# Moving the scaled sum of the fetched V rows from ScalarE and GpSimd to one VectorE instruction

## The chip, the core and the metric

The kernel runs on one core of one Trainium2 chip. The metric is device time in microseconds (us) of one execution. The engines are named PE (TensorE: matrix products; PEld is its weight load), DVE (VectorE), ACT (ScalarE), POOL (GpSimd) and SP (SyncE, which only issues DMAs here). Each engine runs its own instructions strictly in the order in which the program lists them.

## What is computed

One layer of a decoder: two mixing branches, an expert mixer called PEER and an embedding step, over 544 tokens of width 2048. The change lies in PEER. Cut to it, the reference is:

```python
q = (xt @ w_q).reshape(n, PEER_HEADS, 2, D_KEY // 2)
s = jnp.einsum('nhpd,hpkd->nhpk', q, sub_keys)
...                                   # top 16 of 128 keys, twice; top 16 of their sums: idx, g
hb = jax.nn.gelu(jnp.einsum('chkd,cd->chk', u[ib], xb))
return jnp.einsum('chk,chkd->cd', (hb * gb), v[ib])
```

Each token picks 16 experts in each of 8 heads, 128 picks out of 16384 experts. A pick's row of `u` is dotted with the token, the result goes through a gelu and is multiplied by the pick's gate, and the pick's row of `v`, scaled by that number, is added to the token's output.

## The kernel before

The 544 tokens are columns. All weights go through one pipeline of 764 units (`run_units`), a unit being a 128 x 1024 block of weights. SP loads it (tile `wr`), ACT rounds it to a high part `wh` (L224), DVE subtracts to get the low part `wl` (L225), both two units ahead of PE, and PE runs 8 k-tiles with three products each (L280 where 416 columns are used, L284 for 544). `wh` and `wl` have three buffers each.

PEER treats the tokens in two ways. The first 416 (`DC`) meet all experts in dense products: 256 units with U (the U stage), then 256 units with V (the V stage). In the U stage an epilogue per pair of units multiplies on DVE (L1092), takes a gelu on ACT (L1093) and stores to `Hd`. The last 128 tokens (`NS`) have their rows fetched: for each of the 128 picks POOL issues an indirect DMA (L1039) that brings one row of `u` per token, 128 x 2048 numbers, and later one of `v`. A U row is multiplied with the tokens and summed on DVE (L1046, into column i of `hsp`). A V row is scaled by `hsp` on ACT (L1052) and added into `vacc` on POOL (L1053) for picks below 96. For the last 32 picks one DVE instruction does both (L1055). V rows of a batch of 32 come one batch behind U rows, one of each in turn. The fetched rows have three buffers. They lie in the tile `raw` in the U stage and in `gb` in the V stage; a V row's sum always goes to `vacc`, which is part of `raw`.

Beside the dense U products runs other side work: top-16 searches on DVE (`tk1`), the choice of the picks (`tk2`), and for the dense tokens the building of a gate table. One step of that table compares on DVE (tiles `ob` and `oa`, L997 and L999), multiplies `ob` twice by the gates on POOL (L1001), runs 8 small products on PE (L974, into a PSUM tile `aux` with two buffers), and copies them out on ACT (L976, into `gst`). After 8 steps ACT sends `gst` (2 MB) to `Gd` in memory.

The order of all this is fixed when the program is built. `run_units` calls `side()` twice per unit. Each call is a tick. It adds `pace["sp"]` to a debt, and when the debt reaches 1 a fetched row is used (`sp_step`). It adds `pace["main"]` (in us of DVE work) to another debt and runs steps of the side work, each with a cost written beside its `yield` (0.5 where none stands), until that debt is used up. What `sp_step` returns is taken off the same debt. `PACE_U` holds the two numbers for the U stage, `PACE_V` those for the V stage, where the first is so large that it never limits. 24 units before the end of the U stage `gates_done` runs whatever side work is left at once.

Of the kernel before, what the change touches and what calls it, by code (L numbers as in the profile page):

```python
# [17 lines left out]
P = 128  # L18
D = 2048
KT = D // P  # L20
NP = 512            # prompt tokens
NB, ND = 8, 4       # sample batch, tokens per sequence
T = NP + NB * ND    # token columns: prompt, then (b, t)
HB = T // 2
LP = 568            # columns of the recurrence layout: prompt, 3 spare, then (b, 7)
LH = LP // 2
RN = 8              # recurrence tiles
EPS = 1e-6
NEG = -1e30
NS = P              # last token columns, whose experts' rows are fetched one by one  # L30
DC = T - NS         # token columns that meet all experts in dense products
TC = 32             # tokens per chunk of the gate scratch
NCH = DC // TC
NW = 24             # operand pairs of the second PEER product
QB = 4
# [5 lines left out]
GS = 32768.0  # L41
PACE_U, PACE_V = (1.256, 0.243), (1e6, 0.34)
NWA = 2 * KT * T // (2 * DC)    # of these, the pairs that lie in the activations' space


def _token_tiles(t0, t1):
    """Tiles of nt tokens with ng head groups on the partitions: row = group * nt + token."""
    out = []
    while t0 < t1:
        nt = next(n for n in (128, 64, 32) if n <= t1 - t0)  # L50
        out.append((t0, nt, P // nt))
        t0 += nt
    return out
# [13 lines left out]
def _build(ctx, tc, nc, I, O):  # L67
# [9 lines left out]

# [1 line left out]
    def const(name, shape):  # L79
# [15 lines left out]

# [1 line left out]
    AH, AL = [None] * KT, [None] * KT  # L97
# [16 lines left out]

    # sum of squares of the raw columns, folded to 1/rms of every column on every partition
    ssum = {}

    def sq_add(k, pool, x=0):
        """x: whose sum it joins, VectorE's or GpSimd's (which squares for itself)"""
        new = x not in ssum  # L120
        if new:
            ssum[x] = misc[:, (4 + x) * T:(5 + x) * T]
        s = ssum[x] if new else pool.tile([P, T], F32, name="sq", tag=f"sq{x}", bufs=2 - x)
        if x:
            GP.tensor_mul(s, raw[:, k, :], raw[:, k, :])
        else:
            A.activation(s, raw[:, k, :], AF.Square)
        if not new:
            (GP if x else V).tensor_add(ssum[x], ssum[x], s)
# [12 lines left out]

# [1 line left out]
    LOADA, SPLITA = 4, 2  # L144
# [3 lines left out]
    def side():  # L148
        """A part of the work beside the products: steps worth pace["main"] us of the vector engine."""
        SPS["tick"] = SPS.get("tick", 0) + 1  # L150
        owed["sp"] += pace["sp"]
        if owed["sp"] >= 1:
            owed["sp"] -= 1
            owed["main"] -= sp_step()
        owed["main"] = min(owed["main"] + pace["main"], 2 * pace["main"])
        while owed["main"] > 0:
            c, more = advance()
            owed["main"] -= c
            if not more:
                break  # L160
# [4 lines left out]
    def unit(src, groups, **kw):  # L165
        """src: [128, 8, 128]; groups: (accumulator key, [(kl, operand getter)], start, stop, epilogue)"""
        units.append(dict(src=src, groups=groups, **kw))

    def gemm(src, ops, epi, nk=2, cols=None, **kw):
        """One output tile: nk half chunks of 8 k tiles, operands ops(k)."""  # L170
        key = object()
        for hc in range(nk):
            last = hc == nk - 1
            unit(src(hc), [(key, [(kl, (lambda k=hc * 8 + kl: ops(k))) for kl in range(8)], hc == 0, last,
                            epi if last else None)], cols=cols, **(kw if last else {}))
# [3 lines left out]
    def advance():  # L179
        cost, more = 0.0, bool(active or gens)  # L180
        while len(active) < maxact[0] and gens:
            if gens[0] is None:      # what follows needs everything before it
                if active:
                    break
                gens.popleft()
                continue
# [111 lines left out]

# [1 line left out]
    pa = ExitStack()  # L300
# [29 lines left out]

    # RG-LRU branch
    L = {}
# [9 lines left out]
    def decay_rate():  # L342
        # sp4 = 4 * softplus(-lam), with log1p kept accurate for small arguments
        t = [pL.tile([P, RN], F32, name=f"sp{i}") for i in range(6)]
# [95 lines left out]

    # attention branch
    Q = {}
# [189 lines left out]

# [1 line left out]
    W = I["w_in"]  # L634
# [10 lines left out]

# [1 line left out]
    pld = [dram.tile([P, T], F32, name=f"pl{j}") for j in range(KT)]  # L647
    plx = []

    def start_ple():  # L650
        for k in range(2):
            t = pL.tile([P, T], F32, name="pin", tag="pin", bufs=2)
            SP.dma_start(out=t, in_=I["pT"][k])
            h, l = act_tile(KT - 2 + k)      # free until the last operands of w_in are split
            split_to(h, l, t)
# [42 lines left out]

# [1 line left out]
    B = {}  # L700
# [48 lines left out]
    Hd = [dram.tile([P, DC], F32, name=f"Hd{e}") for e in range(P)]  # L749
    NGB = 3             # buffers of fetched rows  # L750
    idx, gsp, hsp = (cst.tile([P, P], dt, name=nm)
# [54 lines left out]

# [1 line left out]
    def epi_pq(j, acc):  # L808
# [44 lines left out]
    def tk1(ti, q):  # L853
# [16 lines left out]
        V.tensor_copy(TK["x1f"][:, 2 * q:2 * q + 2], x1)  # L870
        # pairs (a, b) of ranks with (a + 1)(b + 1) <= 16 hold the 16 best: a = 0, then 1..7 with b < 8,
        # then 8..15 with b = 0, in the order of the flat index
        cd = pU.tile([P, 2, 80], F32, name="cd", tag="cd", bufs=2)
# [12 lines left out]
    def tk2(ti):  # L886
# [4 lines left out]
        x1f, ts, sel = TK["x1f"][:, :nh], TK["ts"][:, :nh], TK["sel"][:, :nh]  # L891
        # ranks (a, b) of every pick, from its place among the pairs
        hu = pU.tile([P, 2, P], U32, name="hu", tag="hu", bufs=1)
# [16 lines left out]
        yield 2.4  # L910
        # the chosen key pair of every pick
        for x in range(2):
            for h2 in range(0, nh, 2):
# [11 lines left out]
                yield 1.8  # L925
        # gates
        g = pk[:, 2, :n].rearrange("p (h j) -> p h j", h=nh)
# [19 lines left out]
        for x in range(3):  # L947
            if ng == 1:
                PE.transpose(ps[:, 0, x * P:x * P + nt], pk[:, x, :], ident)
                continue  # L950
            # rows (group, token) to rows (group, pick): every group's picks in columns of its own
            ex = pU.tile([P, ng, n], F32, name="ex", tag="ex", bufs=2)
# [8 lines left out]
        yield  # L961
        # a gate, times GS to keep it in float16's range, as the sum of two float16
        g16 = pU.tile([P, P], F16, name="g16", tag="mk", bufs=1)
# [46 lines left out]

    # the fetched experts: one pick of every row of a sparse tile at a time, the rows of U against the
    # tokens on the vector engine, those of V, a batch later, into the sums on GpSimd
    BT = 32
# [29 lines left out]
    def sp_use():  # L1043
        kind, i, t, _ = fl.popleft()
        if kind == "u":
            V.scalar_tensor_tensor(t, t, 1.0, xtok, op0=ALU.mult, op1=ALU.mult, accum_out=hsp[:, i:i + 1])  # L1046
            if i % BT == BT - 1:
                b = slice(i - BT + 1, i + 1)
                A.activation(hsp[:, b], hsp[:, b], AF.Gelu_apprx_tanh)
                V.tensor_mul(hsp[:, b], hsp[:, b], gsp[:, b])  # L1050
        elif i < P - BT:
            A.activation(t, t, AF.Copy, scale=hsp[:, i:i + 1])  # L1052
            GP.tensor_add(vacc, vacc, t)  # L1053
        else:
            V.scalar_tensor_tensor(vacc, t, hsp[:, i:i + 1], vacc, op0=ALU.mult, op1=ALU.add)  # L1055

    def sp_step():
        sp_issue()
        cost = 0.0
        if fl and SPS["tick"] - fl[0][3] >= TKD:  # L1060
            cost = 2.3 if fl[0][0] == "u" else 0.0
            sp_use()
# [86 lines left out]
    def wfirst():  # L1149
        """Products for the first group; the operands that fit beside U's."""  # L1150
        gload(0)
# [17 lines left out]
    def wsecond():  # L1169
        """In place of the first half of U's operands."""  # L1170
        drain()
# [31 lines left out]
    def weave(n=3):  # L1203
        """The first halves of the last n tiles, then the second halves."""
        units[-2 * n:] = units[-2 * n::2] + units[1 - 2 * n::2]
# [32 lines left out]

    # operands of the last product go where the last group's W leave room, in the order that they leave
    def klass(p):  # L1240
# [27 lines left out]
    def post_first(g, lo, hi):  # L1268
        """The first halves of the last tiles are through: their operands' place is free."""
        def f():  # L1270
# [38 lines left out]

# [1 line left out]
    def pre_c(j):  # L1311
# [137 lines left out]
```

## Time and profile before

| | |
|---|---|
| time, median of 3 runs | 4259.7 us (4259.34 to 4266.0) |
| span of the profiled execution | 4266.4 us |
| PE busy in the span | 4122.2 us (97%) |
| DVE busy | 2807.7 us (66%) |
| ACT busy | 1534.6 us (36%) |
| POOL busy | 1224.6 us (29%) |
| U stage (1516.7 to 2901.0 us) | 1384.3 us |
| V stage (2901.0 to 4065.0 us) | 1164.0 us |

The profiled execution's own time is its span, 6.7 us above the median. PE is the engine that the rest feeds, so the table's first question is where PE is idle or runs at less than the full granted clock, and the second is which engine's instruction ended that idle time. Both stages multiply the same number of 416-column products, so their difference is a first measure of what PE loses in the U stage.

### The profile page before, as it was taken

What the parts mean: (1) busy time and instruction counts of PE and PEld (TensorE: products, weight loads), DVE (VectorE), ACT (ScalarE), POOL (GpSimd) and SP (SyncE); (2) the same over time, 40 slices, a digit from 0 to 9 for tenths busy, and PEclk for the clock granted to TensorE, in tenths of its full rate; (3) what the DMA queues carried; (4) which work ended last, traced back from release to release, by engine and by line L of the source; (5) the groups of instructions that cost most, each with busy time, mean ns of one, the idle gap of its engine ahead of it and who ended that gap; (6) DMA issues with size and microseconds to landing.
All of it is one profiled execution on the core that took longest, in us unless ns stands there. A gap on an engine that the chain in (4) does not pass through costs nothing.

```text
span 4266.4 us, 63247 instructions
## 1 busy us (share of the span) xinstructions
PE 4122.2 (97%) x26089; PEld 4024.8 (94%) x26089; DVE 2807.7 (66%) x3659; ACT 1534.6 (36%) x1799; POOL 1224.6 (29%) x723
## 2 busy tenths in 40 slices
PE   7999999999999999999888988889999999999999
PEld 7999999999999999999878988889999999999999
DVE  7755444233434369888887988757888878877443
ACT  4442334321223233343343344334444444332331
POOL 3000000000000001464485377413555555410000
PEclk9999999999999999999999999999999999999999
DMA  5232232243343347677666666668989888997333
GB/s 180 80 125 79 75 106 86 84 135 134 124 131 104 111 144 266 234 274 254 215 231 213 233 209 217 224 221 289 332 312 332 326 315 314 323 327 248 118 131 102
DMA packets 323154, 848.69 MB, mean 199 GB/s; under 512 B 26409, under 2 KB 170729, under 8 KB 290097
## 3 DMA queue, kind: packets, MB, share of 16 engines
q1 hardware_dynamic: 204960, 492.69, 34.3%
q0 software_dynamic: 44864, 295.20, 18.6%
q10 hardware_dynamic: 73040, 56.76, 4.0%
q8 instruction: 204, 3.34, 0.3%
q14 instruction: 86, 0.70, 0.0%
HBM read 760.78 MB, written 83.77 MB: 198 GB/s over the span
## 4 chain that ended last, share of the span: by engine, by line
PE 85%; DVE 9%; ACT 2%; issue 2%; DMA 1%; ACTq 1%; POOL 0%; SPq 0%; DVEq 0%
PE acc L280 45%; PE acc L284 36%; DVE wl L225 4%; DVE raw L1046 1%; PE aux L974 1%; ACTq L1094 1%; ACT wh L224 1%; DVE misc L1092 1%; PE aux L519 1%; ACT gst L976 1%; PE aux L556 1%; DMA Gd<-gst 0%; PE aux L284 0%; ACT misc L1093 0%; PE aux L836 0%
## 5 line engine op out<-in xcount | busy, mean ns | idle before, releaser
L225 DVE TENSOR_TENSOR wl<-wr,wh 128x1024 fp32r<-128x1024 f32 x764 | 1220.6, 1599 | 1291.3 <-ACT wh L224 1287.7
L280 PE MATMUL acc<-opf,wh 128*128 128x416 f32 x7424 | 2038.5, 356 | 0.9 <-ACT wh L224 0.9
L280 PEld LDWEIGHTS acc<-opf,wh 128*128 128x128 f32 x7424 | 1405.4, 191 | 16.5 <-ACT wh L224 1.8
L224 ACT ACTIVATE wh<-wr 128x1024 fp32r<-128x1024 f32 x764 | 805.0, 1058 | 1577.9 <-PE acc L284 801.3
L284 PE MATMUL acc<-opf,wh 128*128 128x272 f32 x7936 | 1348.9, 292 | 22.3 <-ACT wh L224 9.1
L280 PE MATMUL acc<-opf,wl 128*128 128x416 f32 x3712 | 1316.5, 355 | 52.1 <-DVE wl L225 52.0
L284 PEld LDWEIGHTS acc<-opf,wh 128*128 128x128 f32 x7936 | 1140.7, 190 | 36.0 <-issue 15.1
L284 PE MATMUL acc<-opf,wl 128*128 128x272 f32 x3968 | 827.7, 290 | 0.0
L280 PEld LDWEIGHTS acc<-opf,wl 128*128 128x128 f32 x3712 | 708.8, 191 | 68.4 <-DVE wl L225 62.8
L284 PEld LDWEIGHTS acc<-opf,wl 128*128 128x128 f32 x3968 | 628.5, 189 | 0.3 <-DVE wl L225 0.3
L1001 POOL TENSOR_TENSOR ob<-ob,gh 128x512 f16<-128x512 f16 x208 | 313.1, 1510 | 71.2 <-DVE ob L997 60.1
L1053 POOL TENSOR_TENSOR raw<-raw,gb 128x2048 f32<-128x2048 f32 x59 | 276.8, 4692 | 124.2 <-ACT gb L1052 123.9
L1093 ACT ACTIVATE misc<-misc 128x416 f32<-128x416 f32 x128 | 70.6, 552 | 573.1 <-DVE misc L1092 573.1
L1039 POOL DMA_INDIRECT gb<-i_vn,idx x91 | 115.9, 1274 | 384.2 <-DVE gb L1046 222.5
L1053 POOL TENSOR_TENSOR raw<-raw 128x2048 f32<-128x2048 f32 x37 | 177.8, 4805 | 161.6 <-ACT raw L1052 161.6
L280 PE MATMUL acc<-wx,wh 128*128 128x416 f32 x768 | 206.8, 350 | 0.0
L1046 DVE SCALAR_TENSOR_TENSOR raw<-raw,misc 128x2048 f32<-128x2048 f32 x69 | 172.8, 2504 | 0.0
L1039 POOL DMA_INDIRECT raw<-i_un,idx x69 | 104.7, 1517 | 231.7 <-DVE raw L1046 153.5
L644 POOL DMA_DIRECT2D sg<-sgt x32 | 17.4, 543 | 510.3 <-ACT sgt L643 510.3
L280 PEld LDWEIGHTS acc<-wx,wh 128*128 128x128 f32 x768 | 143.8, 187 | 1.4
L1046 DVE SCALAR_TENSOR_TENSOR gb<-gb,misc 128x2048 f32<-128x2048 f32 x59 | 134.4, 2279 | 0.0
L280 PE MATMUL acc<-wx,wl 128*128 128x416 f32 x384 | 134.2, 349 | 0.0
(299 smaller groups left out, 2915.2 us busy)
## 6 DMA issues: line engine op xcount, KB each, us to landing
wr<-i_u SPq DMA_DIRECT2D x256, 512.0 KB
wr<-i_v SPq DMA_DIRECT2D x256, 512.0 KB
wr<-i_w_in SPq DMA_DIRECT2D x120, 512.0 KB
Hd<-misc ACTq DMA_DIRECT2D x128, 208.0 KB
Gd<-gst ACTq DMA_DIRECT2D x13, 2048.0 KB
gt<-Gd SPq DMA_DIRECT2D x32, 832.0 KB
misc<-Hd SPq DMA_DIRECT2D x112, 208.0 KB
wr<-i_w_proj SPq DMA_DIRECT2D x32, 512.0 KB
```

The source lines that it names most:

```text
L224: A.activation(hit[u], r, AF.Copy)
L225: V.tensor_sub(lot[u], r, hit[u].bitcast(F32))
L280: PE.matmul(acc[:, 0, :ncol], lhsT=w[:, kl, :], rhs=x[:, :ncol], start=st and t == 0, stop=sp and t == 2)
L284: PE.matmul(acc[:, s, :HB], lhsT=w[:, kl, :], rhs=x[:, s * HB:(s + 1) * HB], start=st and t == 0, stop=sp and t == 2)
L519: PE.matmul(sc[:, g, j0:], lhsT=raw[hs, RN + 4 * kp + g, blk * P:(blk + 1) * P], rhs=Q["k", kp][hs, ks:ks + nk], start=True, stop=True)
L556: PE.matmul(ps[hs, 0, :], lhsT=Q["v", kp][:, blk - 1 + kb, hs], rhs=pt[:, kb, :], start=kb == kbs[0], stop=kb == 1)
L974: PE.matmul(pq[:, q], lhsT=oa[:, q, :], rhs=ob[:, q, x, :], start=x == 0, stop=x == 1)
L1001: GP.tensor_tensor(out=ob[:, :, x, :], in0=ob[:, :, 0, :], in1=gh[:, x, tk, None].to_broadcast([P, 4, P]), op=ALU.mult)
L1039: GP.indirect_dma_start(out=t, out_offset=None, in_=I[kind + "n"], in_offset=bass.IndirectOffsetOnAxis(ap=idx[:, i:i + 1], axis=0))
L1046: V.scalar_tensor_tensor(t, t, 1.0, xtok, op0=ALU.mult, op1=ALU.mult, accum_out=hsp[:, i:i + 1])
L1053: GP.tensor_add(vacc, vacc, t)
L1093: A.activation(h, h, AF.Gelu_apprx_tanh)
```

## The change

Every V row is now scaled and added by the DVE instruction that served the last 32 picks. ACT's scaling (L1052) and POOL's add (L1053) are gone for the other 96. `sp_step` now returns 2.3 for V rows too, and the U stage's pace of side work goes from 1.256 to 1.4 per tick. The rest of the diff deletes comments, which moves line numbers by three (the multiply-add is L1052 in the new kernel, the epilogue's multiply L1089).

```diff
-PACE_U, PACE_V = (1.256, 0.243), (1e6, 0.34)
+PACE_U, PACE_V = (1.4, 0.243), (1e6, 0.34)
...
                 V.tensor_mul(hsp[:, b], hsp[:, b], gsp[:, b])
-        elif i < P - BT:
-            A.activation(t, t, AF.Copy, scale=hsp[:, i:i + 1])
-            GP.tensor_add(vacc, vacc, t)
         else:
             V.scalar_tensor_tensor(vacc, t, hsp[:, i:i + 1], vacc, op0=ALU.mult, op1=ALU.add)
...
         if fl and SPS["tick"] - fl[0][3] >= TKD:
-            cost = 2.3 if fl[0][0] == "u" else 0.0
+            cost = 2.3
             sp_use()
```

Three places show how the order moves. The first is POOL at the point in the U stage where row fetching has been switched on and the first gate steps come. Before:

```order
L943 MEMSET raw 128x2048
L1039 DMA raw<-i_un,idx 128x2048 x17
L1001 TENSOR_TENSOR ob<-ob,gh 128x4x128 x6
L1039 DMA raw<-i_un,idx 128x2048
L1001 TENSOR_TENSOR ob<-ob,gh 128x4x128 x2
```

After:

```order
L943 MEMSET raw 128x2048
L1039 DMA raw<-i_un,idx 128x2048 x14
L1001 TENSOR_TENSOR ob<-ob,gh 128x4x128 x8
L1039 DMA raw<-i_un,idx 128x2048 x2
L1001 TENSOR_TENSOR ob<-ob,gh 128x4x128 x6
```

The gate steps now begin three U rows (seven units) earlier, and more of them stand between two fetches.

The second place is POOL in the middle of the U stage, where U and V rows take turns beside gate steps. Before:

```order
L1039 DMA raw<-i_vn,idx 128x2048
L1001 TENSOR_TENSOR ob<-ob,gh 128x4x128 x4
L1053 TENSOR_TENSOR raw<-raw 128x2048
L1039 DMA raw<-i_un,idx 128x2048
L1039 DMA raw<-i_vn,idx 128x2048
L1001 TENSOR_TENSOR ob<-ob,gh 128x4x128 x6
L1053 TENSOR_TENSOR raw<-raw 128x2048
```

After:

```order
L1001 TENSOR_TENSOR ob<-ob,gh 128x4x128 x2
L1039 DMA raw<-i_vn,idx 128x2048
L1001 TENSOR_TENSOR ob<-ob,gh 128x4x128 x6
L1039 DMA raw<-i_un,idx 128x2048
L1001 TENSOR_TENSOR ob<-ob,gh 128x4x128 x4
L1039 DMA raw<-i_vn,idx 128x2048
L1001 TENSOR_TENSOR ob<-ob,gh 128x4x128 x4
```

The adds are gone from POOL. It keeps the fetches and the gate multiplies.

The third place is DVE in the same part of the U stage, three to four units of each kernel; before, a V row's turn lies in it but shows no instruction on DVE. Before:

```order
L225 TENSOR_TENSOR wl<-wr,wh 128x1024
L997 TENSOR_TENSOR ob<-iota,pkT 128x4x128
L999 TENSOR_TENSOR oa<-iota,pkT 128x512
L225 TENSOR_TENSOR wl<-wr,wh 128x1024
L1092 TENSOR_TENSOR misc<-acc,rs 128x416
L225 TENSOR_TENSOR wl<-wr,wh 128x1024
L997 TENSOR_TENSOR ob<-iota,pkT 128x4x128
L999 TENSOR_TENSOR oa<-iota,pkT 128x512
L225 TENSOR_TENSOR wl<-wr,wh 128x1024
L1092 TENSOR_TENSOR misc<-acc,rs 128x416
L1046 SCALAR_TENSOR_TENSOR raw,hsp<-raw,misc 128x2048
```

After:

```order
L225 TENSOR_TENSOR wl<-wr,wh 128x1024
L1052 SCALAR_TENSOR_TENSOR raw<-raw,hsp 128x2048
L225 TENSOR_TENSOR wl<-wr,wh 128x1024
L1089 TENSOR_TENSOR misc<-acc,rs 128x416
L997 TENSOR_TENSOR ob<-iota,pkT 128x4x128
L999 TENSOR_TENSOR oa<-iota,pkT 128x512
L225 TENSOR_TENSOR wl<-wr,wh 128x1024
L997 TENSOR_TENSOR ob<-iota,pkT 128x4x128
L999 TENSOR_TENSOR oa<-iota,pkT 128x512
L1046 SCALAR_TENSOR_TENSOR raw,hsp<-raw,misc 128x2048
```

A V row is now one DVE instruction of 2048 elements, two units from the nearest U row's, and the tick that runs it has no gate step.

## Rows read from the trace of the kernel before

**Rows 1.** Busy times by stretch: no V rows yet, V rows, V stage.

```profile
core 0: us, PE busy (x) PEld busy (x) DVE busy (x) ACT busy (x) POOL busy (x), PEclk, DMA share, GB/s
1516.70:1965.00 448.30, 445.45 (x2551) 436.34 (x2552) 364.62 (x615) 170.01 (x189) 165.91 (x110) 1.00 0.69 240
1965.00:2901.00 936.00, 826.47 (x4483) 790.30 (x4482) 750.00 (x1073) 362.51 (x383) 488.49 (x250) 0.94 0.65 221
2901.00:4065.00 1164.00, 1161.52 (x6164) 1149.45 (x6163) 901.04 (x808) 454.30 (x473) 477.10 (x207) 1.00 0.82 294
```

**Rows 2.** The same columns, two stretches of the U stage before any V row.

```profile
1605.00:1712.00 107.00, 107.00 (x575) 106.71 (x575) 101.06 (x254) 32.10 (x36) 16.69 (x11) 1.00 0.71 256
1712.00:1926.00 214.00, 211.31 (x1250) 204.98 (x1249) 173.20 (x173) 85.59 (x97) 117.35 (x78) 0.99 0.76 258
```

**Rows 3.** PE's waits from 1965 to 2901 us: waiter, releaser, total, times, longest.

```profile
PE acc L280 <- DVE wl L225: 49.5, 24, 4.5
PE aux L974 <- ACT gst L976: 48.8, 17, 5.4
PE aux L974 <- POOL ob L1001: 7.8, 5, 2.9
PE aux L956 <- DVE ex L955: 3.4, 3, 2.6
```

**Rows 4.** POOL, then DVE, in order of time, 2530 to 2540 us: start, duration.

```profile
2531.60 4.62 POOL L1053 TENSOR_TENSOR raw<-raw 128x2048 f32<-128x2048 f32 x1 [2.09 <-ACT raw L1052]
...
2532.50 4.80 DVE L225 TENSOR_TENSOR wl<-wr,wh 128x1024 fp32r<-128x1024 f32 x1 [1.62 <-ACT wh L224]
2537.22 0.58 DVE L1092 TENSOR_TENSOR misc<-acc,rs 128x416 f32<-128x416 f32 x1
```

**Rows 5.** PE in order of time, 2535 to 2549.6 us, its idle time in brackets.

```profile
2537.35 0.46 PE L280 MATMUL acc<-opf,wl 128*128 128x416 f32 x1 [0.87 <-DVE wl L225]
...
2549.54 0.29 PE L974 MATMUL aux<-ob,oa 128*128 128x128 f16 x1 [5.27 <-ACT gst L976]
```

**Rows 6.** DVE, then ACT, in order of time, 2540 to 2552 us.

```profile
2541.08 2.28 DVE L1046 SCALAR_TENSOR_TENSOR raw<-raw,misc 128x2048 f32<-128x2048 f32 x1
...
2544.50 2.46 DVE L225 TENSOR_TENSOR wl<-wr,wh 128x1024 fp32r<-128x1024 f32 x1
2546.88 0.58 DVE L1092 TENSOR_TENSOR misc<-acc,rs 128x416 f32<-128x416 f32 x1
...
2547.49 0.55 ACT L1093 ACTIVATE misc<-misc 128x416 f32<-128x416 f32 x1 [5.34 <-DVE misc L1092]
```

**Rows 7.** Busy times by stretch again: that gap, and after it.

```profile
2544.00:2549.50 5.50, 0.27 (x2) 0.00 (x0) 5.50 (x6) 1.61 (x3) 4.77 (x4) 0.79 0.88 316
2549.50:2556.00 6.50, 6.46 (x29) 6.27 (x30) 6.50 (x5) 4.58 (x4) 6.34 (x5) 0.65 0.32 115
```

**Rows 8.** Groups of DVE, 963 to 1070 us (POOL idle): count, busy us, mean ns.

```profile
L225 DVE TENSOR_TENSOR wl<-wr,wh 128x1024 fp32r<-128x1024 f32 x18 | 22.1, 1226 | 69.1 <-ACT wh L224 69.1
```

**Rows 9.** The same view, 1712 to 1926 us (gate steps and U rows, no add).

```profile
L225 DVE TENSOR_TENSOR wl<-wr,wh 128x1024 fp32r<-128x1024 f32 x44 | 67.1, 1525 | 35.3 <-ACT wh L224 35.3
L1046 DVE SCALAR_TENSOR_TENSOR raw<-raw,misc 128x2048 f32<-128x2048 f32 x21 | 55.2, 2628 | 0.0
L997 DVE TENSOR_TENSOR ob<-iota,pkT 128x512 f16<-128x512 f32 x28 | 24.4, 873 | 0.0
L999 DVE TENSOR_TENSOR oa<-iota,pkT 128x512 f16<-128x512 f32 x28 | 21.6, 770 | 0.0
```

**Rows 10.** The same view, 1965 to 2887 us (with adds).

```profile
L225 DVE TENSOR_TENSOR wl<-wr,wh 128x1024 fp32r<-128x1024 f32 x160 | 333.6, 2089 | 174.8 <-ACT wh L224 174.6
L1046 DVE SCALAR_TENSOR_TENSOR raw<-raw,misc 128x2048 f32<-128x2048 f32 x35 | 87.6, 2503 | 0.0
L997 DVE TENSOR_TENSOR ob<-iota,pkT 128x512 f16<-128x512 f32 x72 | 84.5, 1173 | 0.0
L999 DVE TENSOR_TENSOR oa<-iota,pkT 128x512 f16<-128x512 f32 x72 | 77.6, 1078 | 0.0
```

**Rows 11.** The same view, V stage.

```profile
L225 DVE TENSOR_TENSOR wl<-wr,wh 128x1024 fp32r<-128x1024 f32 x256 | 442.7, 1730 | 226.5 <-ACT wh L224 223.9 <-PE acc L280 2.0
L1055 DVE SCALAR_TENSOR_TENSOR raw<-gb,hsp,raw 128x2048 f32<-128x2048 f32 x32 | 75.0, 2343 | 0.0
```

**Rows 12.** The removed instructions, whole span: U stage (raw<-raw), V stage (gb).

```profile
L1053 POOL TENSOR_TENSOR raw<-raw,gb 128x2048 f32<-128x2048 f32 x59 | 276.8, 4692 | 124.2 <-ACT gb L1052 123.9
L1053 POOL TENSOR_TENSOR raw<-raw 128x2048 f32<-128x2048 f32 x37 | 177.8, 4805 | 161.6 <-ACT raw L1052 161.6
L1052 ACT ACTIVATE gb<-gb,hsp 128x2048 f32<-128x2048 f32 x59 | 117.6, 1994 | 0.0
L1052 ACT ACTIVATE raw<-raw,hsp 128x2048 f32<-128x2048 f32 x37 | 74.0, 2000 | 25.9 <-issue 17.9 <-ACT misc L1093 5.7 <-ACT gst L976 2.3
```

## The prediction

> **What bounds the kernel now.** I read the stretches first [rows 1]. PE has no slack in the V stage: 1161.5 us busy in 1164.0, at the full granted clock. The U stage does the same number of wide products, plus the small ones of the gate table, and takes 1384.3 us (448.3 + 936.0). PE is busy for 445.5 + 826.5 = 1271.9 us of that, so it is idle for 112.4 us. Nearly all of it, 109.5 us, lies after 1965 us, where V rows have begun. There the mean granted clock is 0.94, which means that PE spent part of the stretch at 1.2 instead of 2.4 GHz. That costs 0.06 x 936 = 56 us of full-speed time. Some of it falls into the gaps themselves: in one gap of 5.5 us the clock falls (0.79) with PE busy for 0.3 us, and the next 6.5 us run at 0.65 [rows 7]. I take 50 us as the clock's price, 0.45 us for each us of gap. So PE loses some 162 us in the U stage, and that is all that a better order of the other engines can win.
>
> Who ends the gaps: 49.5 us wait for `wl` on DVE, 48.8 us for ACT's copy of the gate products, 7.8 us for POOL's gate multiply, 3.4 us for another DVE step [rows 3]. DVE is 80% busy there (750.0 of 936.0). But it is 81% busy from 1712 to 1926 us, with gate steps and a U row every two units, and there PE loses 2.7 us in 214; from 1605 to 1712 us it is 94% busy and PE loses nothing [rows 2]. So DVE's total load is not what hurts. What is new after 1965 us is POOL's add of a V row. At 2531.60 us such an add runs for 4.62 us, and a `wl` that began inside it takes 4.80 us and ends just after it [rows 4], where an undisturbed one takes 1.226 us [rows 8]. PE then waits for that `wl`. The second long gap, 5.27 us, comes 12 us later [rows 5]: DVE is behind, a U row of 2.28 us and a `wl` of 2.46 us stand in front of the epilogue L1092, ACT waits 5.34 us for that, and the copy that PE needs stands behind ACT's wait [rows 6].
>
> **The change part by part: U stage.** Per stretch the group means give what adds cost DVE, taking the no-add stretch as the base, since gate multiplies on POOL disturb DVE in both [rows 9, 10]: `wl` (2089 - 1525) x 160 = 90 us, `ob` (1173 - 873) x 72 = 22 us, `oa` (1078 - 770) x 72 = 22 us. That is 134 us for 36 adds in the stretch, 3.7 us each, and the single case of rows 4 gives 4.80 - 1.23 = 3.6. Removing 37 adds takes about 135 us of DVE time away. The new multiply-add exists already, 32 times in the V stage at 2343 ns [rows 11]; 37 of them are 87 us. Where POOL's gate multiplies overlap, it will look like the U rows, whose mean is 2503 to 2628 ns [rows 9, 10], so 87 to 97 us. DVE wins about 40 us, and the disturbances become smaller: 2.3 us at a planned place instead of 3.7 us wherever the add falls. ACT loses 37 x 2.0 = 74 us and POOL 178 us of work [rows 12]. I cost both at nothing beyond the gaps already counted: neither is 55% busy in any stretch of rows 1.
>
> POOL's queue: a fetch stood behind its V row's add and now waits for DVE's instruction, and the gate multiplies stand behind that fetch. A U row's fetch waits like this today. DVE runs its queue in order, so the multiply's `ob` comes after the same row anyway; cost nothing, and the cover that could be lost is the 7.8 us class of rows 3.
>
> The pace: 512 ticks x 0.144 = 74 us more side work is allowed, and 37 x 2.3 = 85 us is taken off for V rows. Over the stage that cancels. It is not even: before V rows start (88 units, 176 ticks) DVE gets 25 us more, 364.6 + 25 = 390 of 448 us, or 87%. Afterwards it gets less work per tick than now. A row every two units with DVE near 87% is what the whole U stage becomes, and rows 2 are its nearest neighbours on both sides, 81% and 94%.
>
> How much gap stays? Low end: the rate of the no-add stretch, 2.7 us in 214, over a stage of some 1230 us: 15 us. High end: the 60 us that rows 3 give to other things than `wl` stay whole, plus the 2.9 us before 1965: 63 us. I take 35. It is nearer the low end, because the gaps of the second class also follow adds (rows 4 to 6), and above it, because each unit carries 2 x 0.144 = 0.29 us more DVE work than in that stretch and the leftover gate steps are still run in one go near the end. Then 112 - 35 = 77 us of gaps and 77 x 0.45 = 35 us of clock are won: 112 us. The ends give (112 - 15) x 1.45 = 141 and (112 - 63) x 1.45 = 71 us.
>
> **V stage.** `wl` alone loses (1730 - 1226) x 256 = 129 us to adds today [rows 8, 11], and 59 multiply-adds of 2343 ns bring 138 us. DVE stays near its 77% (901 of 1164). PE's idle time is 2.5 us, so at most that is won. Bound on the loss: the no-add rate of rows 2 over 1164 us, 15 us. I take 0, since adds that hold `wl` for 3.6 us do no harm there now.
>
> One rule speaks against the change. An instruction of this form with two fp32 sources took 2343 ns for 2048 elements [rows 11], 1.14 ns each, against 1.20 ns for the two-source subtraction [rows 8]. The Trainium skill, "Vector Engine (DVE) Microarchitecture Reference", section "Points that are easy to get wrong", says that a scalar-tensor-tensor with two SBUF sources that are not bf16 runs at half throughput. By that rule a V row would be an estimated 4.7 us, 174 us in the U stage, more than the 135 us removed, and the gain would be gone. The 32 rows measured in this kernel show no halving, so the sum goes by them.
>
> **Sum.** Against the profiled execution: 4266.4 - 112 + 0 = 4154 us. That execution lies 6.7 us above the median of the runs, so 4148; I say **4150**, with 4120 to 4190 from the ends above.
>
> **The rivals.** *The lumps are exchanged in part.* The ACT class of gaps needs no add, only a long DVE instruction ahead of the epilogue, and a V row now is one. Today 35 U rows go with 48.8 us of that class, 1.4 us each. If the 60 us stay and V rows add half of 37 x 1.4, 26 us, gaps are 63 + 26 = 89, the win is 23 x 1.45 = 34 us: 4225. For it: rows 6 show a U row in exactly that place. Against: rows 2, with a row every two units and almost no gaps. *Exchanged in full:* 52 us instead of 26, gaps 115: 4260, no change.
>
> *Slower: the raised pace makes the early part fall behind.* Its place is units 220 to 307, between 1517 and 1965 us. If DVE there reaches the state of the later stretch (109.5 us of gaps in 936, 0.117 per us), 448 us bring 52 instead of 2.9 us of gaps, 49 x 1.45 = 71 us, on top of the full exchange: 4330; half of it, 4295. It decides when DVE's work between two `wl` exceeds the time of a unit on PE for many units in a row. 87% is short of that, but 94% in rows 2 consists of small instructions, which the gate steps and rows are not.
>
> **How the numbers follow.** Forecast 0.70, partial exchange 0.18, full exchange 0.05, slower 0.07. That the change does not happen is no case: the order shows no add left on POOL. The range takes the forecast with a margin of 15 us on the low side and reaches to the middle of the partial exchange: 4105 to 4225, which leaves out half of that rival (0.09), the other two (0.12) and little more. A difference under 0.2% (8.5 us) cannot be told from no change here. Faster by more: 0.70 + 0.18 = 0.88; within: 0.05; slower: 0.07.
>
> **What would show it.** In the new profile, right: no `wl` of 4.6 to 4.9 us anywhere; PE's waits for `wl` in the U stage below 15 us and for ACT's gate copy below 30; the U stage near 1270 us with a granted clock of 0.98 or more; the V stage at 1164 within 5; the multiply-add at 2.34 us in the V stage and up to 2.6 in the U stage. Wrong: ACT's gate copy keeps its 50 us or grows and each gap follows a V row's multiply-add (exchange), new gaps between 1517 and 1965 us (pace), or PE idle in the V stage.

## The result, and the profile after

The changed kernel takes 4189.42 us, the median of 4 runs (4187.95 to 4196.22), against 4261.35 us (4 runs, 4259.34 to 4266.0) for the kernel before in the same session: a ratio of 0.9827, interval 0.9814 to 0.9841 (the quotient of the two medians, 0.9831, lies inside it). The prediction was 4150, range 4105 to 4225. The time lies in the range and the sign is right, but the gain is 72 us, not 110: the time is at the slow end of the forecast's own 4120 to 4190, and halfway to the rival of 4225. One of the four runs of the pace alone, below, took 8551.29 us and is counted in the median given there; without it that median is 4294.5 us. The profiled execution is one of 4187.95 us with a span of 4186.2, 80.2 us less than that of before.

The first line of the page of the kernel after gives busy time, share of the span and instructions of each engine:

```profile
PE 4086.4 (98%) x26089; PEld 4001.9 (96%) x26089; DVE 2710.2 (65%) x3755; ACT 1358.7 (32%) x1703; POOL 726.8 (17%) x627
```

ACT lost 176 us of work, POOL 498 us (455 of them its adds [rows 12]), and DVE, which took the work over, lost 97.5 us as well. Where the 80.2 us were won shows in the stretches. Columns are as in [rows 1]: stretch, length, then busy time of PE, PEld, DVE, ACT and POOL, granted clock, DMA share, GB/s. First the U stage of the kernel before as one stretch, then, of the kernel after, the U stage, the V stage, and the U stage in two parts, without and with V rows.

```profile
1516.70:2901.00 1384.30, 1271.92 (x7032) 1226.64 (x7033) 1114.61 (x1687) 532.52 (x572) 654.40 (x359) 0.96 0.66 227
...
1515.10:2823.60 1308.50, 1237.12 (x7032) 1203.62 (x7033) 1065.63 (x1724) 464.21 (x535) 469.07 (x322) 0.98 0.69 240
2823.60:3985.00 1161.40, 1161.40 (x6165) 1150.47 (x6165) 852.32 (x867) 346.91 (x414) 165.02 (x148) 1.00 0.83 295
1516.70:1965.00 448.30, 427.32 (x2420) 415.04 (x2420) 372.44 (x710) 156.99 (x180) 153.28 (x106) 0.98 0.67 231
1965.00:2820.00 855.00, 804.63 (x4588) 783.41 (x4587) 689.34 (x1010) 305.46 (x353) 315.79 (x216) 0.97 0.71 246
```

The U stage went from 1384.3 to 1308.5 us [rows 1], which is 75.8 of the 80.2; the V stage won 2.6 us. Within the U stage, for the same 7032 matmul records, PE's busy time fell from 1271.9 to 1237.1: 34.8 us, which I put down to the clock (granted 0.96 before, 0.98 after). Its idle time fell from 112.4 to 71.4 us: 41.0 us. The early part got worse. Between 1516.7 and 1965 us PE stood idle for 2.9 us before [rows 1], and now for 448.3 - 427.3 = 21.0 us, though the stretch has hardly a V row: the kernel after begins its first at 1964.8 us, and the kernel before has the add of its first there, at 1945.13, and the start of the second's, at 1963.79.

PE's waits in the U stage, in the columns of [rows 3] (waiter, releaser, total us, times, longest), and the line of ACT's waits that grew most:

```profile
PE aux L974 <- ACT gst L976: 50.7, 15, 9.7
PE aux L974 <- POOL ob L1001: 16.2, 10, 2.9
...
PE acc L280 <- DVE wl L225: 2.0, 3, 1.4
...
ACT gst L976 <- DMA Gd<-gst: 42.7, 6, 11.7
```

The 49.5 us for `wl` in [rows 3] are 2.0. The 48.8 us for ACT's gate copy are still 50.7. ACT's wait for the store of `gst` was 7.2 us in 6 times in the kernel before:

```profile
ACT gst L976 <- DMA Gd<-gst: 7.2, 6, 2.7
```

The groups of DVE answer to [rows 10] and [rows 11]: line, operation, tiles, shape, count, then busy us, mean ns, and idle time before. Five are from 1965 to 2820 us, two from the V stage:

```profile
L225 DVE TENSOR_TENSOR wl<-wr,wh 128x1024 fp32r<-128x1024 f32 x166 | 239.3, 1443 | 153.8 <-ACT wh L224 153.8
L1052 DVE SCALAR_TENSOR_TENSOR raw<-raw,hsp 128x2048 f32<-128x2048 f32 x37 | 94.8, 2562 | 0.0
L1046 DVE SCALAR_TENSOR_TENSOR raw<-raw,misc 128x2048 f32<-128x2048 f32 x36 | 87.2, 2422 | 0.0
L997 DVE TENSOR_TENSOR ob<-iota,pkT 128x512 f16<-128x512 f32 x72 | 69.5, 965 | 0.0
L999 DVE TENSOR_TENSOR oa<-iota,pkT 128x512 f16<-128x512 f32 x72 | 61.7, 857 | 0.0
...
L225 DVE TENSOR_TENSOR wl<-wr,wh 128x1024 fp32r<-128x1024 f32 x256 | 313.6, 1225 | 279.7 <-ACT wh L224 277.9
L1052 DVE SCALAR_TENSOR_TENSOR raw<-gb,hsp,raw 128x2048 f32<-128x2048 f32 x91 | 213.4, 2345 | 0.0
```

`wl` fell from 2089 to 1443 ns in the U stage and from 1730 to 1225 ns in the V stage. Over both stages no `wl` is longer than 2499 ns; this line of the view of L225 has the shortest, median and longest duration of the 512:

```profile
L225 DVE TENSOR_TENSOR wl<-wr,wh x512: 1204/1226/2499, 1515.1 to 3981.5; 128x1024 fp32r<-128x1024 f32 x171
```

The gaps that remain are of two kinds. The longest, 9.66 us, is of the first. Rows in order of time (start, duration, idle time before in brackets): ACT, where ACTq is the issue of a DMA, then the PE instruction that ends the gap.

```profile
2224.79 0.38 ACTq L978 DMA_DIRECT2D Gd<-gst  x1
...
2232.05 6.89 ACTq L1091 DMA_DIRECT2D Hd<-misc  x1
2242.06 1.02 ACT L976 ACTIVATE gst<-aux 128x512 f32<-128x512 f32 x1 [10.04 <-DMA Gd<-gst]
...
2243.14 1.03 PE L974 MATMUL aux<-ob,oa 128*128 128x128 f16 x8 [9.66 <-ACT gst L976]
```

The 2 MB store of `gst` is issued at 2224.79, and the copy that waits for it starts 17.3 us later. `gst` has one buffer, so the first copy of the next chunk waits for it, the two `aux` buffers of PE stay full, and PE stops behind them. The issue of the small `Hd` store, on the same engine, takes 6.89 us in between instead of its usual 0.33.

The second kind has a fetched row in it. DVE, then PE and ACT, at 2086 us:

```profile
2083.73 2.34 DVE L1052 SCALAR_TENSOR_TENSOR raw<-raw,hsp 128x2048 f32<-128x2048 f32 x1
2085.99 0.69 DVE L997 TENSOR_TENSOR ob<-iota,pkT 128x512 f16<-128x512 f32 x1
2086.59 0.68 DVE L999 TENSOR_TENSOR oa<-iota,pkT 128x512 f16<-128x512 f32 x1
2087.20 2.45 DVE L225 TENSOR_TENSOR wl<-wr,wh 128x1024 fp32r<-128x1024 f32 x1
2089.57 0.58 DVE L1089 TENSOR_TENSOR misc<-acc,rs 128x416 f32<-128x416 f32 x1
...
2092.23 1.03 PE L974 MATMUL aux<-ob,oa 128*128 128x128 f16 x8 [5.68 <-ACT gst L976]
...
2090.19 0.55 ACT L1090 ACTIVATE misc<-misc 128x416 f32<-128x416 f32 x1 [5.76 <-DVE misc L1089]
```

A V row, a gate step and a `wl` of 2.45 us stand ahead of the epilogue L1089, ACT waits 5.76 us for that, and the copy that PE needs stands behind ACT's wait. It is the pattern of [rows 6], with a V row where a U row was. Gap by gap, the 50.7 us read so: three gaps of 9.22, 9.52 and 9.66 us end with a copy that had waited 10 us or more for the store, 28.4 us together. Behind a U row stand 4.41, 3.11 and 1.99 us, 9.5 together. Behind a V row stand the 5.68 shown and one of 2.31 us, 8.0 together. The other seven are 4.8 us in all.

### The profile page after: what moved, and what is told of

The parts are those of the page before. It is cut to its first block, busy times and chain, and to the rows that moved or that the text cites. A ratio compares the mean times of both kernels' runs of the same rounds, so it can differ in the third digit from the quotient of the medians.

```text
span 4186.2 us, 62977 instructions
## 1 busy us (share of the span) xinstructions
PE 4086.4 (98%) x26089; PEld 4001.9 (96%) x26089; DVE 2710.2 (65%) x3755; ACT 1358.7 (32%) x1703; POOL 726.8 (17%) x627
## 3 DMA queue, kind: packets, MB, share of 16 engines
q1 hardware_dynamic: 204960, 492.69, 34.9%
## 5 line engine op out<-in xcount | busy, mean ns | idle before, releaser
L225 DVE TENSOR_TENSOR wl<-wr,wh 128x1024 fp32r<-128x1024 f32 x764 | 989.2, 1296 | 1321.2 <-ACT wh L224 1318.5
L280 PE MATMUL acc<-opf,wl 128*128 128x416 f32 x3712 | 1301.2, 351 | 2.0 <-DVE wl L225 2.0
L1052 DVE SCALAR_TENSOR_TENSOR raw<-gb,hsp,raw 128x2048 f32<-128x2048 f32 x91 | 213.4, 2345 | 0.0
L1039 POOL DMA_INDIRECT gb<-i_vn,idx x91 | 100.5, 1104 | 503.1 <-DVE gb L1046 318.8
L1039 POOL DMA_INDIRECT gb<-i_un,idx x59 | 66.5, 1126 | 434.1 <-DVE raw L1052 328.9
L976 ACT ACTIVATE gst<-aux 128x512 f32<-128x512 f32 x104 | 112.7, 1110 | 72.7 <-DMA Gd<-gst 42.7
L974 PEld LDWEIGHTS <-oa 128*128 128x128 f16 x832 | 49.4, 101 | 89.2 <-ACT gst L976 66.9
```

Source lines behind the costliest of these rows:

```text
L225: V.tensor_sub(lot[u], r, hit[u].bitcast(F32))
L280: PE.matmul(acc[:, 0, :ncol], lhsT=w[:, kl, :], rhs=x[:, :ncol], start=st and t == 0, stop=sp and t == 2)
L974: PE.matmul(pq[:, q], lhsT=oa[:, q, :], rhs=ob[:, q, x, :], start=x == 0, stop=x == 1)
L976: A.activation(gst[:, :, q0:q0 + 4].rearrange("p i q -> p q i"), pq, AF.Copy, scale=1.0 / GS)
L1039: GP.indirect_dma_start(out=t, out_offset=None, in_=I[kind + "n"], in_offset=bass.IndirectOffsetOnAxis(ap=idx[:, i:i + 1], axis=0))
```

## The experiments

The theory after the result: the adds' hold on DVE is gone, as predicted, and what was given back came in with the pace, which packs the gate steps so that ACT meets its own store. The rival: the V rows themselves, now on DVE, make the new gaps. The kernels ran in three sessions beside runs of the kernel before (medians 4266.44, 4266.9 and 4265.94 us), so they are compared by their ratios to it, and a difference of ratios is turned into us with 4266.

**The pace alone, and the move alone.** The kernel before with the new pace and the cost of 2.3 for V rows, whose adds stay on POOL:

```diff
-PACE_U, PACE_V = (1.256, 0.243), (1e6, 0.34)
+PACE_U, PACE_V = (1.4, 0.243), (1e6, 0.34)
...
-            cost = 2.3 if fl[0][0] == "u" else 0.0
+            cost = 2.3
```

> The kernel before with the change's two planning numbers alone (pace 1.4, 2.3 counted for V rows); V rows stay on ScalarE and GpSimd. The order of the side work is then that of the kernel after, and only where V rows run differs. If GpSimd's adds holding VectorE is the cause, PE's waits for wl stay near 50 us in the U stage and the time near 4260 us (4240 to 4280). If the better-spread side work is the cause, the time comes near the kernel after, 4190 to 4210 us, with few waits for wl.

Measured: 4295.61 us, ratio 1.0068 (1.0048 to 1.0088), 29 us slower than before. The stretch without V rows, and PE's waits from 1515 to 2924 us, the U stage's end here:

```profile
1516.70:1965.00 448.30, 427.00 (x2420) 414.91 (x2419) 372.12 (x709) 156.81 (x179) 153.24 (x106) 0.98 0.67 231
```

```profile
PE aux L974 <- ACT gst L976: 63.0, 17, 8.7
PE acc L280 <- DVE wl L225: 46.6, 20, 4.1
```

The early stretch is that of the kernel after to within 0.3 us (427.00 and 427.32 busy), so its new gaps come from the pace. The waits for `wl` stay, so the pace does not remove them. The changed kernel with the old pace:

```diff
-PACE_U, PACE_V = (1.4, 0.243), (1e6, 0.34)
+PACE_U, PACE_V = (1.256, 0.243), (1e6, 0.34)
```

> The kernel after with the old pace of 1.256: the move of the V rows alone, with their 2.3 us taken off the side work. By its order, 23 gate steps instead of 4 are left to be run in one go at the end of the U stage. If the adds' hold is the cause, PE's waits for wl vanish (under 10 us); the 19 more leftover steps cost about 2 us each as the last four do, 40 us, so about 4230 us (4200 to 4250). If the pace brings the gain, it stays at 4260 us, with the wl waits still there.

Measured: 4201.93 us, ratio 0.9846 (0.9829 to 0.9862). The early stretch, a stretch late in the U stage, and a part of PE's and ACT's waits from 1515 to 2839 us:

```profile
1516.00:1965.00 449.00, 445.94 (x2554) 436.78 (x2555) 367.98 (x618) 167.17 (x188) 159.09 (x109) 1.00 0.69 242
...
2690.00:2760.00 70.00, 41.72 (x232) 39.70 (x233) 51.41 (x87) 21.11 (x27) 22.09 (x16) 0.71 0.50 155
```

```profile
PE acc L280 <- DVE wl L225: 1.2, 2, 0.8
...
ACT gst L976 <- DMA Gd<-gst: 57.2, 7, 12.6
```

Here the early part loses 3.1 us, and the waits for `wl` are gone without any help from the pace. But V rows are now taken off the debt, so less side work gets done per tick: 23 gate steps are left for the run at the end, and PE is idle for 28.3 us of the 70 around it at a clock of 0.71. ACT's wait for the store is 57.2 us, more than the 42.7 of the kernel after, and all but 0.8 of it comes after 1965 us. So the long store waits late in the stage don't need the new pace. The two kernels together split the change: at the new pace the move is worth 1.0068 - 0.9827, 103 us; the pace costs 29 us on the old kernel, and on the new one it wins 8 us or nothing (the intervals overlap), since it trades 28 us of idle time in the leftover run, of which 8 remain, for 18 us of early gaps.

**What holds DVE.** The kernel before without POOL's add, so that the sum lacks the V rows below pick 96; ACT still scales them:

```diff
-            GP.tensor_add(vacc, vacc, t)
```

> The kernel before without GpSimd's adds: the V rows below 96 are fetched and scaled but not summed, so that part of the output is missing. Pace and order of the rest are those of before. If the adds' hold is the cause, PE's waits for wl fall below 10 us and the time to 4150 to 4190 us, since VectorE has neither the hold nor the new instruction. If ScalarE's scaling or the side work's place matters more, 4230 us or above. The V stage should not change by more than 5 us either way.

Measured: 4162.19 us, ratio 0.9754 (0.9738 to 0.977), 105 us less than before. Waits of PE and ACT from 1515 to 2798 us, and `wl`'s group from 1965:

```profile
PE aux L974 <- ACT gst L976: 42.5, 16, 9.1
...
PE acc L280 <- DVE wl L225: 0.6, 1, 0.6
...
ACT gst L976 <- DMA Gd<-gst: 28.5, 8, 11.9
```

```profile
L225 DVE TENSOR_TENSOR wl<-wr,wh 128x1024 fp32r<-128x1024 f32 x162 | 224.7, 1391 | 203.2 <-ACT wh L224 202.9
```

The waits for `wl` are gone, with nothing on DVE in the adds' place. But PE still waits 42.5 us for ACT's copy, and its waits add up to 52.5 us, without an add, without a multiply-add below pick 96 and at the old pace. So that class of gaps doesn't need adds. And ACT's wait for the store rose from 7.2 to 28.5 us with no edit but this one.

Is it the add's time on POOL, or what it reads? In the next kernel three fills of the fetched row stand in the add's place, longer together than an add, and write only; the sum lacks the same rows.

```diff
-            GP.tensor_add(vacc, vacc, t)
+            for _ in range(3):
+                GP.memset(t, 0.0)
```

> The kernel before with each of GpSimd's adds replaced by three GpSimd fills of the same 128 x 2048 buffer, which write but read nothing (the one fill in the trace took 1.83 us, so three are 5.5 us against the add's 4.7); the sum of those V rows is missing. If what holds VectorE is that the add reads its operands from the on-chip memory, the fills hold nothing: no wl above 2.6 us, waits for wl under 10 us, and the time of the run without adds, 4162 us, within 20. If any GpSimd work on that memory holds VectorE, or GpSimd's queue being late is the cause, the time is 4260 us or above.

Measured: 4172.58 us, ratio 0.9777 (0.9761 to 0.9793), 95 us less than before, though POOL works longer on a row than with the adds. `wl` from 1965 to 2840 us, and one set of fills (POOL) with the `wl` that DVE ran beside it:

```profile
L225 DVE TENSOR_TENSOR wl<-wr,wh 128x1024 fp32r<-128x1024 f32 x170 | 232.3, 1370 | 217.1 <-ACT wh L224 210.5 <-ACT gh L966 3.2 <-ACT gst L976 1.6
```

```profile
2100.17 5.55 POOL L1054 MEMSET raw<- 128x2048 f32 x3
...
2103.94 1.22 DVE L225 TENSOR_TENSOR wl<-wr,wh 128x1024 fp32r<-128x1024 f32 x1 [2.14 <-ACT wh L224]
```

A `wl` inside the 5.55 us of fills takes 1.22 us, where one inside an add of 4.62 us took 4.80 [rows 4]. So time on POOL alone does not hold DVE, and the add does. The fills differ from it in two things, that they read nothing and that they add nothing; no run here separates the two. The Trainium skill, "SBUF — State Buffer", section "Summary: rules for kernel authors", says that a VectorE instruction with two SBUF inputs and a GpSimd instruction that reads SBUF exclude each other, the second waiting until the first is through. The two rows agree with that.

**The V stage.** The changed kernel, with ACT and POOL doing the V rows below pick 96 again in the V stage only:

```diff
+        elif SPS["vphase"] and i < P - BT:
+            A.activation(t, t, AF.Copy, scale=hsp[:, i:i + 1])
+            GP.tensor_add(vacc, vacc, t)
```

> The kernel after with the V rows of the V stage back on ScalarE and GpSimd, those of the U stage on VectorE. The prediction costs the V stage's part of the change at nothing: the time of the kernel after, 4189 us, within 6. If adds cost the V stage something that the trace of before does not show as waits of PE, it is slower than that by more than 8 us.

Measured: 4190.62 us, ratio 0.9824 (0.9808 to 0.9841): the same time. In the V stage `wl` is held again, and PE's only waits there are these:

```profile
L225 DVE TENSOR_TENSOR wl<-wr,wh 128x1024 fp32r<-128x1024 f32 x256 | 437.0, 1707 | 227.1 <-ACT wh L224 226.7
```

```profile
PE acc L280 <- DVE wl L225: 2.1, 2, 1.5
```

So the move is worth nothing in the V stage, though adds hold `wl` there too, and all of the gain is the U stage's.

**What a row costs in the U stage.** A second multiply-add per V row of the U stage, writing over the fetched row, which is no longer used:

```diff
+            if not SPS["vphase"]:
+                V.scalar_tensor_tensor(t, t, hsp[:, i:i + 1], vacc, op0=ALU.mult, op1=ALU.add)
```

> The kernel after with each multiply-add of the U stage followed by a second one of the same size that writes into the row's own buffer and is not used: 37 x 2.3 to 2.6 us, 85 to 96 us more VectorE work at the same places. If VectorE still has slack there and the rest of the gaps is the gate store, it costs little, under 15 us. If each row's multiply-add is a lump that delays the epilogue and with it ScalarE's gate copy (the rival of the prediction), the price doubles too: 1.4 us a row and its clock, 40 to 90 us, 4230 to 4280 us.

Measured: 4259.21 us (10 runs), ratio 0.9984 (0.9975 to 0.9994). That is 0.0157 or 67 us more than the kernel after, for 37 instructions of 2441 ns: 1.8 us of the end time each, clock included. PE's waits from 1515 to 2899 us:

```profile
PE aux L974 <- ACT gst L976: 72.6, 21, 12.5
PE acc L280 <- DVE wl L225: 23.1, 21, 2.8
```

A row's multiply-add in the U stage is by no means free. About half of the new gaps are the rival's mechanism: those for ACT's copy went from 50.7 to 72.6 us. The other half the rival did not name: PE waits for `wl` itself, 23.1 us against 2.0. The 1.8 us are a marginal price, of a second instruction right behind the first. The first ones cost less. The kernel without adds runs none for these rows, at the old pace, and the kernel after is slower than it by 0.9827 - 0.9754, 31 us. That is for the 37 multiply-adds and the new pace and costs together, 0.8 us a row.

**The store's wait, taken away.** `GW` is the number of side-work steps that the first copy of a chunk is put off behind the store of the chunk before. A second buffer of `gst` would remove the wait as such and was not tried. With `GW` at 6, at the pace of after and at 1.5 to leave less over:

```diff
-GW = 3
+GW = 6
```

> The kernel after with the wait of 6 ticks alone, pace 1.4 as in the kernel after; by its order 8 instead of 4 gate steps and six more searches are left over at the end of the U stage. The store's waits vanish (under 5 us of ScalarE's 42.7). If they were the cause of their gaps, some 30 us of gaps go and the longer leftover costs 10 to 15 back: 4160 to 4180 us. If the gaps come back as waits behind rows, 4185 us or more.

```diff
-GW = 3
+GW = 6
...
-PACE_U, PACE_V = (1.4, 0.243), (1e6, 0.34)
+PACE_U, PACE_V = (1.5, 0.243), (1e6, 0.34)
```

> The kernel after with 6 instead of 3 ticks between the store of a gate chunk and the first step of the next (one buffer for both), and a pace of 1.5 so that the table is still done in time (by its order, no step is left over). If the rest of the gaps in the kernel after is ScalarE waiting for that store to land (42.7 us, the long gaps of 5.7 to 9.7 us), those vanish with the 8 us of leftover steps: 45 us of gaps and some clock, about 4135 us (4120 to 4155). If the rest is VectorE's rows standing in front of the epilogue, the higher pace makes it worse: 4190 to 4220 us.

Measured: 4182.89 us, ratio 0.9807 (0.979 to 0.9823), and 4181.78 us, ratio 0.9802 (0.9786 to 0.9818). Both lie 9 to 11 us under the kernel after, and their intervals overlap with its. ACT's wait for the store is 3.5 us in the first and 1.3 in the second, down from 42.7. Net, taking 40 us of that wait away was worth a quarter of it. PE's waits in the U stage, of the first and then of the second:

```profile
PE aux L974 <- POOL ob L1001: 25.5, 10, 7.6
PE aux L974 <- ACT gst L976: 20.8, 13, 4.3
PE aux L956 <- DVE ex L955: 15.9, 3, 15.2
```

```profile
PE aux L974 <- ACT gst L976: 31.8, 11, 7.3
PE acc L280 <- DVE wl L225: 19.8, 19, 3.0
```

In the first, the gaps for ACT's copy fell by 30 us, from 50.7 to 20.8, as expected of the store. But the delays use up side steps, so gate steps are left over again: 17.5 of its 25.5 us and all of the 15.9 lie between 2680 and 2760 us, where the kernel after loses 7.9. The leftover cost 25 us and not the 10 to 15 expected. The second finishes the steps in time, with the store's wait gone, and still has 31.8 us of gaps for ACT's copy and 19.8 for `wl`; its higher pace is the one difference to the first. So the store does make gaps, and my theory that it alone was the cause of the missing gain fell here: remove its wait and the load shows elsewhere.

**Less load in the U stage.** In the V stage PE has no waits to speak of, so fewer rows are used in the U stage and more in the V stage, alone and with `GW` at 6:

```diff
-PACE_U, PACE_V = (1.4, 0.243), (1e6, 0.34)
+PACE_U, PACE_V = (1.4, 0.17), (1e6, 0.43)
```

> The kernel after with the row pace alone changed (0.17 in the U stage, 0.43 in the V stage); 3 ticks after a store as before. It splits the gain of the run with fewer rows (4143 us). If rows in front of the epilogue are the larger part, most of the gain is here: 4145 to 4160 us. If the store is, ScalarE still waits some 40 us for it and PE with it: 4165 to 4185 us.

```diff
-GW = 3
+GW = 6
...
-PACE_U, PACE_V = (1.4, 0.243), (1e6, 0.34)
+PACE_U, PACE_V = (1.4, 0.17), (1e6, 0.43)
```

> The kernel after with 6 ticks between a gate chunk's store and the next chunk, and the row pace lowered in the U stage (0.17) and raised in the V stage (0.43), so that some 32 rows move from the U stage to the V stage, where PE has no waits. By its order no gate step is left over. If both the store and the rows in front of the epilogue make the rest of the gaps, they fall to some 30 us: 4130 us (4110 to 4155). If the V stage cannot take the rows (VectorE or the fetches too late there), PE waits in the V stage and the time is 4190 us or above.

Measured: 4171.11 us, ratio 0.9768 (0.9752 to 0.9784), and 4143.47 us, ratio 0.9712 (0.969 to 0.9733). Against the kernel after that is 25 us for the rows alone, about 9 for `GW` alone, and 49 for both. That is 15 us more than the sum, about as much as the intervals leave open. It would fit that with room on DVE the side work that `GW` puts off is done in time. A step further, with a lower pace:

```diff
-GW = 3
+GW = 6
...
-PACE_U, PACE_V = (1.4, 0.243), (1e6, 0.34)
+PACE_U, PACE_V = (1.3, 0.14), (1e6, 0.46)
```

> The run with fewer rows taken one step further: row pace 0.14 and 0.46, side pace 1.3, 6 ticks after a store; no gate step left over. The U stage's remaining waits (some 25 us) fall with VectorE's load, the V stage keeps PE fed if its slack holds: 4125 to 4140 us. If the V stage is the limit, its PE waits grow past 10 us and the time stays above 4145.

Measured: 4125.37 us (4121.61 to 4130.5), ratio 0.9666 (0.965 to 0.9682): the fastest kernel here, 69 us below the kernel after. The U stage, PE's wait for ACT's copy in it, and the rows used in it from 1965 us on:

```profile
1515.00:2752.70 1237.70, 1220.50 (x7033) 1188.18 (x7034) 978.21 (x1658) 469.63 (x535) 415.37 (x278) 1.00 0.64 217
```

```profile
PE aux L974 <- ACT gst L976: 7.2, 6, 3.3
```

```profile
L1046 DVE SCALAR_TENSOR_TENSOR raw<-raw,misc 128x2048 f32<-128x2048 f32 x27 | 68.9, 2550 | 0.0
L1052 DVE SCALAR_TENSOR_TENSOR raw<-raw,hsp 128x2048 f32<-128x2048 f32 x15 | 37.2, 2483 | 0.0
```

With 15 V rows and 27 U rows instead of 37 and 36, gaps for ACT's copy fall from 50.7 to 7.2 us, and PE's idle time in the U stage from 71.4 to 17.2 us. Four numbers were changed here at once, so what each is worth is not shown. The V stage does pay a little: PE waits there for 8.0 us (4.3 for `wl`, 3.7 for `wh`), where the kernel after has no waits.

## Why the prediction was right in its sign and too large in its size

*The adds' hold: right.* It was put at 135 us of DVE time in the U stage. `wl` lost (2089 - 1443) x 166 = 107 us, `ob` (1173 - 965) x 72 = 15 us and `oa` (1078 - 857) x 72 = 16 us, 138 us in all; no `wl` of 4.6 us is left, and PE's wait for `wl` is 2.0 us. Removing the add alone is worth 105 us of end time.

*The multiply-adds: their duration right, their price wrong.* 37 x 2562 ns = 94.8 us, inside the 87 to 97 stated, and 2345 ns in the V stage. The halving that the prediction weighed and set aside did not come, now on 91 rows of the V stage and not on 32. What was not right is that a row at a planned place costs the path next to nothing: a second one costs 1.8 us each, and the first ones with the new pace 0.8. The rival "exchanged in part" took 0.7 us of gap per V row, on the grounds of [rows 6]. Its mechanism is there at 2086 us, but only 8.0 us of the gaps stand right behind a V row. It was set aside by [rows 2], where a row every two units leaves almost no gaps, but those rows are from a stretch without V rows and at the old pace.

*The pace: a step that failed.* "Over the stage that cancels" was costed at nothing. The sum of the work does cancel, its place does not: the new pace costs the early part 21.0 - 2.9 = 18 us (the kernel with the pace alone shows the same 21), and 29 us in all on the old kernel. The slower rival named that place and took 49 us for it, so it was real and a third of its size. The 87% of DVE were reckoned rightly: 372.4 us for 2420 products are 392.6 for the 2551 of before, against 390 foreseen, and the 83% of the clock time (372.4 of 448.3) come of PE's idling. What was wrong is that 87% would bring no gaps. PE's wait for ACT's copy there and ACT's for the store, then ACT's for the store in the same stretch of the kernel after with the old pace:

```profile
PE aux L974 <- ACT gst L976: 16.2, 4, 9.2
...
ACT gst L976 <- DMA Gd<-gst: 13.9, 2, 11.7
```

```profile
ACT gst L976 <- DMA Gd<-gst: 0.8, 1, 0.8
```

The gap of 9.2 us is the store's, about half of the 18 us; one of 4.4 us comes behind a U row, before the first store. With `GW` at 6 alone, PE's idle time there is 449 - 437.57 = 11.4 us. The prediction named no store; in the trace of before it was a wait of 7.2 us on an engine that was 36% busy.

*The gaps left: the mis-sized term, and the reason that failed.* 35 us were predicted, 71.4 measured, above the stated high end of 63, which did not hold the pace's term. Half of the miss is the pace's 18 us. Behind most of the rest is the reason given for a value near the low end, that the gaps of the second class "also follow adds". They don't: without any add the class is still 42.5 us in the U stage, against 51.4 before (48.8 of them in [rows 3]). With the adds gone ACT meets its own store instead: its wait for it is 28.5 us in that kernel, 42.7 in the kernel after and 57.2 with the move alone, against 7.2 before. The pace alone, with the adds in place, brings 34.9. Why the wait comes when the adds go is not shown; it would fit that the holds had put the gate steps further apart. The split of the 50.7 us into 28.4 behind the store and 17.5 behind rows is that of one trace, and not what either is worth: taking one away brings the other, or the leftover, forward.

*The clock: right in sum by luck, wrong in its rate.* 35 us were predicted and 34.8 measured, but for 41 us of gaps and not 77. The rate was 0.85 us per us of gap, not the mean of 0.45. Had it been 0.45, the gain would have been some 16 us smaller. The error in the rate made up for a part of the error in the gaps. Nor is 0.85 a price to carry on: from the kernel after to the fastest one 54.2 us of gaps went and only 16.6 us of PE's busy time, 0.31 for each. What a us of gap costs depends on which gaps go.

*V stage: right; ACT and POOL: not quite nothing.* 1161.4 us against 1164 within 5, and nothing there depends on the move (4190.62 and 4189.42 us). POOL's queue was costed at nothing, and its class went from 7.8 to 16.2 us. Of that, 7.7 us lie in the leftover run between 2680 and 2760 us, but 7.4 of the 7.8 lay in the leftover run before, too. What is new is 2.8 us before 1965 us and two gaps of 2.8 and 2.9 us after it, the first right behind a copy that waited for the store. ACT's wait for the store was not in the sum at all.

Of the signs named in advance, `wl`, the clock, the V stage and the multiply-add's time came out right. The U stage (1308.5 and not 1270 us) and ACT's copy (50.7 and not below 30) did not, and two signs of being wrong came: ACT's copy kept its 50 us, and new gaps came before 1965 us.

## What to carry to other kernels

Work given to another engine can still be paid for by the first: here an add of 4.8 us on POOL cost DVE 3.7 us, and doing it on DVE 2.3 to 2.6. Held time costs only where PE waits for it, in the U stage and not in the V stage. When a change touches both the work and the number that paces it, cost the number by itself: equal sums over a stage say nothing about where the work piles up. Before a class of gaps is said to follow a cause, take the cause away and look at the class: here it stayed. And look for the stage that takes the work for little (8.0 us here) before making room in the one that doesn't.

## What the runs showed of the hardware that was not expected

Three fills on POOL, 5.55 us together, leave a `wl` beside them at 1.22 us, while an add of 4.62 us stretches it to 4.80. That an instruction's time on POOL does not by itself decide was not in the trace of before. And the issue of a 208 KB store on ACT's queue, 0.33 us as a rule, took 6.89 us while the 2 MB store ahead of it on that queue was under way, and another, behind the store issued at 1873.62 us, took 6.93. Of the 13 such issues that come first behind a 2 MB store, a third took 5.49 us, five 0.46 to 1.90, and five the usual time, so the store ahead is not all that decides. The kernel before has it too, with up to 6.50 us. That the one store holds the other's issue was not tried by itself.
